# Moving GpSimd's products of a decoder mixer to VectorE and ScalarE, and the transfers around its triangular solves to ScalarE's queue

## The chip, the cores and the metric

The kernel runs on one core of one Trainium2 chip. Its time is the device time of one launch, in microseconds (us). The engines are named as in the profile: PE is TensorE (matmuls; PEld are its weight loads), DVE is VectorE, ACT is ScalarE, POOL is GpSimd and SP is SyncE, which issues DMA transfers.

## The reference

Two layers (`DEPTH`), 256 tokens, width 1024, f32. Each layer adds four sub-layers to x, each between an RMSNorm before and one after:

```python
x += 0.5 * post(SwiGLU_1(pre(x)))
x += post(W_out[ sum_i sigmoid(gate_i(h)) * U_i(branch_i(h)) ]),  h = pre(x)
#      branch A: latent attention with rotary keys (MLA), causal
#      branch B: gated linear attention (GLA), causal
#      branch C: RWKV-7 time mixing (a delta-rule state), causal
x += post(CrossAttn(pre(x), rmsnorm(mem)))
x += 0.5 * post(SwiGLU_2(pre(x)))
```

The change lies in the second sub-layer, the mixer. Its RWKV branch steps a state per head over the tokens:

```python
sa = state @ kk_t
state = state * w_t - sa x (kk_t * a_t) + v_t x k_t      # x: outer product
y_t = state @ r_t
```

Its GLA branch needs, for all j <= i, the product of q_i, k_j and a decay exp(b_i - b_j), with b a running sum of log gates.

## The kernel before, in words

All 256 tokens stay on the core as two halves of 128 (t = 0 and 1). Matmuls with weights are split in three: each weight block (tile `raw`, by DMA from SP's queue, three buffers) is cut on ACT into a high part (`whi`, a cast) and on DVE into the rest (`wlo`, a subtraction), eight tiles of each; every block then takes part in matmuls high x high, high x low and low x high. Intermediates lie in one big tile cut into buffers (`heap`; `heapr` for split activations; `small` for per-token numbers). PSUM has eight banks: `b_g` and `b_s` for projections and transposes, `b_ya` and `b_yb` for the branches.

Everything is recorded first: every operation becomes an entry of `Program.ops`, and so all compute instructions have the line of `issue` in the profile (L384). `Program.order` then plans: `cost` gives each operation a duration, `forward` simulates the five engines and takes at each one the ready operation of best rank, `backward` makes new ranks from the result, and the best plan of several rounds and passes is issued. The instruction order on every engine comes from these costs and rules, and the buffers in `heap` are laid by the planned times.

RWKV is done in chunks. `rwkv_keys` and `rwkv_products` form products of keys, decays and rates; `rwkv_front` forms, per half, the small matrices (matmuls of 64 contraction rows at two places of the array, `pe` = rows 0 to 63 or 64 to 127) and writes the triangular ones through DRAM (`sl`) into the layout of the solve (`XL`). `rwkv_solve` runs 31 steps on DVE, each a product (`tm`) and a subtraction (`xx`) over 248, 240, ..., 8 columns. The result goes out to DRAM in two layouts (`si`, `sx`) and back into `X1` and `XT`; `rwkv_back` multiplies it into the state. There are four solves: two halves in two layers.

GLA covers the causal triangle in seven levels of block size 64 down to 1 (`gla_attend`): two subtractions on DVE, an exponential on ACT, then the key product (128x256) and two query products into `zq` (64x256 each) on POOL, four matmuls, and an eviction by ACT or, for the four smaller and the last sizes, a predicated copy on DVE. RoPE (`rope`) takes four products and two sums per half. `branch` multiplies each branch's projection by its gate and adds it up (`mg`).

The FFN takes its outer factor 0.5 by a POOL operation on the gain `gb`; `meansq` computes 1/rms of a row.

Of the kernel before, what the change touches and what calls it, by code (L numbers as in the profile page):

```python
# [48 lines left out]
class Program:  # L49
# [139 lines left out]
    @staticmethod  # L189
    def columns(op):  # L190
# [10 lines left out]
    def order(self):  # L201

        self.preds = self.graph()
        ops = self.ops
        n = len(ops)
        self.eng = [o[0].name for o in ops]
        self.costs = [self.cost(o) for o in ops]
        self.succ = [[] for _ in range(n)]
        for i, p in enumerate(self.preds):
            for j in p:  # L210
                self.succ[j].append(i)
        self.size = [o[2][0].nbytes() / self.DMA_RATE if o[0].name == "sync" else 0.0 for o in ops]
# [15 lines left out]
        for i, users in enumerate(self.users):  # L228
            t = self.at[i]
            for b in users:  # L230
                b.start, b.end = min(b.start, t[0]), max(b.end, t[1] + (4.0 if self.eng[i] == "sync" else 0.2))
        return order

    def lag(self, i, s):
        if self.eng[i] == "sync":
            return self.DMA_START + self.size[i] + self.DMA_END
        return self.LAT[self.eng[i]][self.eng[i] != self.eng[s]]
# [36 lines left out]
    def forward(self, rank):  # L274
# [13 lines left out]
        parts, size, place, shared = self.parts, (128, 128), None, False  # L288
        while len(order) < n:
# [23 lines left out]
            if e == "tensor":  # L313
# [9 lines left out]
                if parts[i][0] != size:  # L323
                    j = min((x for x in ready[e] if parts[x[1]][0] == size and x[0] < rank[i] + self.STAY), default=None)
# [7 lines left out]
            if e == "tensor":  # L332
                if parts[i][0] != size:
                    size, shared = parts[i][0], False
                    c += self.DRAIN
                elif size != (128, 128) and not shared and any(
                        a != b for a, b, s in zip(parts[i][1], place, size) if s < 128):
                    shared = True
                    c *= 0.5
                else:  # L340
                    shared = False
# [6 lines left out]
            if e == "tensor":  # L348
# [5 lines left out]
                c *= 1 if warm else 2  # L354
            at[i] = (t, t + c)
# [3 lines left out]
            if e == "sync":  # L359
                dma_free = max(dma_free, t + self.DMA_START) + self.size[i]  # L360
                end = dma_free + self.DMA_END
                done.append(end)
            for s in self.succ[i]:
                rt[s] = max(rt[s], end if e == "sync" else end + self.LAT[e][e != eng[s]])
# [81 lines left out]
class Trunk:  # L446
# [397 lines left out]
    def postnorm(self, y, gb, t):  # L844

        jk, yg, ss = self.h.alloc(D), self.h.alloc(D), self.sm.alloc(2)
        self.meansq(y, jk, ss)
# [13 lines left out]
    def ffn(self, l, i, st, post_g, nxt, after_first=None):  # L861
# [46 lines left out]
        for c in range(1, NCH):  # L908
# [17 lines left out]
        for t in range(2):  # L926
# [3 lines left out]
            self.postnorm(ys[t], gb, t)  # L930
# [71 lines left out]
    def rwkv_keys(self, l):  # L1002
# [34 lines left out]
        for hp in range(4):  # L1037
            self.tt(kmv[:, hp, :], kmv[:, hp, :], k0[:, hp, :], MULT, nc.gpsimd)
        h.free(self.k0)
        for hp in range(4):  # L1040
            self.tt(aa[:, hp, :], aa[:, hp, :], kv[:, hp, :], MULT, nc.gpsimd)

    def rwkv_products(self, l):
# [5 lines left out]
        for hp in range(4):  # L1049
            self.tt(rv[:, hp, :], self.rr.v(f, b=4)[:, hp, :], self.km.v(f, b=4)[:, hp, :], MULT, nc.gpsimd)  # L1050
# [33 lines left out]
    def rwkv_front(self, l, t):  # L1084
# [51 lines left out]
        for q in range(4):  # L1136
            nc.sync.dma_start(sl[q * 8:q * 8 + 8].rearrange("h i j -> i h j"),
                              ln[32 * q:32 * q + 32, :, (q % 2) * 32:(q % 2) * 32 + 32])
        XL, XX = h.alloc(1024), h.alloc(256)
        nc.sync.dma_start(XL.ap, sl.rearrange("b i j -> b (i j)").unsqueeze(1).to_broadcast([32, 4, 1024]))  # L1140
        nc.sync.dma_start(XX.ap, self.ix)
        rt.update(MM=MM, mmv=mmv, PA=PA, BA=BA, pa=pa, ba=ba, LN=LN, ln=ln, XL=XL, XX=XX)

    def rwkv_solve(self, l, t):
# [15 lines left out]
        nc.sync.dma_start(si, XX.ap)  # L1160
        X1 = rt["X1"] = h.alloc(256)
        for q in (0, 2):
            nc.sync.dma_start(X1[32 * q:32 * q + 32, :].rearrange("p (b c) -> p b c", c=8),
                              si.rearrange("(q b) (i c) -> q i b c", q=4, c=8)[q])
        nc.scalar.copy(TM.v("p (c i) -> p c i", c=8), XX.v("p (i c) -> p c i", c=8))
        nc.sync.dma_start(sx, TM.ap)
        xt = XT.v("p (h n) -> p h n", h=8)
        sxv = sx.rearrange("(q h x) (c i) -> q (x c) h i", q=4, h=8, c=8)
        for q in range(4):
            nc.sync.dma_start(xt[32 * q:32 * q + 32, :, 32 * q:32 * q + 32], sxv[q])  # L1170
# [78 lines left out]
    def rwkv_out(self, l, och, ocl):  # L1249
# [7 lines left out]
        for t in range(2):  # L1257
# [11 lines left out]
            self.tt(Y.ap, Y.ap, lw, MULT, nc.gpsimd)  # L1269
            self.tt(Y.ap, Y.ap, lb, ADD, nc.gpsimd)  # L1270
# [3 lines left out]
            self.tt(Y.ap, Y.ap, VN.ap, ADD, nc.gpsimd)  # L1274
# [15 lines left out]
    def rope(self, dst, x1, x2, t, n, eng):  # L1290
# [50 lines left out]
    def mla_up(self, l):  # L1341
# [6 lines left out]
        for t in range(2):  # L1348
# [113 lines left out]
    def gla_attend(self, l, obh, obl):  # L1462
# [48 lines left out]
        for i, L in enumerate((64, 32, 16, 8, 4, 2, 1)):  # L1511
# [9 lines left out]
            self.tt(tv[:, :, 0, :], tv[:, :, 0, :], kv[:, :, 0, :], MULT, nc.gpsimd)  # L1521
            upat = "p (u b x n) -> p u b x n"
            tq, qq = (b.v(upat, u=4, x=2, n=L)[:, :, :, 1, :] for b in (T, QG))
            by_head(Z, lambda pe, z: self.tt(z.rearrange("p u (b n) -> p u b n", n=L), tq[pe], qq[pe], MULT, nc.gpsimd))
# [8 lines left out]
            else:  # L1533
# [19 lines left out]
        for t in range(2):  # L1553
# [13 lines left out]
            self.tt(ov, ov, self.p_gn.unsqueeze(1).to_broadcast([128, 4, 128]), MULT, nc.gpsimd)  # L1567
            self.tt(O.ap, O.ap, gg[t].ap, MULT, nc.gpsimd)
# [14 lines left out]
    def mixer(self, l, st, post_g, nxt):  # L1583
# [258 lines left out]
```

## Time and profile before

| | |
|---|---|
| time, three runs | 1681.28, 1686.76, 1687.56 us (median 1686.76) |
| the profiled execution | 1683.41 us, its span 1681.7 us |
| mean granted TensorE clock | 0.983 |
| busy: PE, DVE, ACT, POOL | 1602.7, 1105.1, 964.1, 268.4 us |
| instructions on POOL | 383 |
| transfers | 274.91 MB, mean 163 GB/s |

A row of a group of instructions names line, engine, operation, output and inputs, shape and count, then the busy time and the mean duration of one in ns, then the idle time of the engine before them and what ended it. A row of waits names who waited for whom, with total us, times and longest. A row of the timeline begins with start and duration in us; the idle time before it stands at its end. A row of a stretch gives the stretch, its length and each engine's busy time with the number of instructions. SPq is SP's queue.

### The profile page before, as it was taken

To read this page: it belongs to the slowest core of one execution; us is meant where nothing else is said; L and a number is where in the kernel's file an instruction comes from. 1 tells how busy PE (TensorE), PEld (TensorE's weight loads), DVE (VectorE), ACT (ScalarE), POOL (GpSimd) and SP (SyncE) were. 2 spreads that over 40 slices of the span, in tenths; PEclk is the share of its full clock that TensorE was granted. 3 is DMA by queue.
4 is the path that set the end of the run, shared out by engine and by line. 5 is a ranking of instruction groups with operands and counts; after the bars stand their busy time and mean duration, and the time that the engine had idled before them with its cause. 6 is when DMAs were issued, how large, how long until landed. Compare 5 with 4: busy or idle time off the path is not lost. (4 is left out here: it accounts for less than half of the span.)

```text
span 1681.7 us, 23946 instructions
## 1 busy us (share of the span) xinstructions
PE 1602.7 (95%) x8623; PEld 1337.0 (80%) x8623; DVE 1105.1 (66%) x1954; ACT 964.1 (57%) x1887; POOL 268.4 (16%) x383
## 2 busy tenths in 40 slices
PE   7999999998899999999999999999978999999998
PEld 5788798776677987888878887887766789878886
DVE  5555656958876667555675557676786776575555
ACT  5455675866445556555555556867854455564544
POOL 7000113105331101000010002310163320010000
PEclk9999999999999999999999999999988999999999
DMA  8655542522555635656555554443225555455652
GB/s 253 207 190 186 171 155 88 169 73 103 170 192 180 206 128 163 202 173 214 174 180 199 193 182 146 131 143 115 91 83 173 175 188 165 149 169 182 199 177 100
DMA packets 206091, 274.91 MB, mean 163 GB/s; under 512 B 28148, under 2 KB 157650, under 8 KB 205972
## 3 DMA queue, kind: packets, MB, share of 16 engines
q1 hardware_dynamic: 205972, 273.39, 50.0%
q8 instruction: 67, 1.10, 0.3%
q14 instruction: 52, 0.43, 0.1%
HBM read 270.60 MB, written 2.75 MB: 163 GB/s over the span
## 5 line engine op out<-in xcount | busy, mean ns | idle before, releaser
L384 DVE TENSOR_TENSOR wlo<-raw,whi 128x512 fp32r<-128x512 f32 (+1 forms) x964 | 673.5, 714 | 401.1 <-ACT whi L384 389.7
L384 ACT CAST whi<-raw 128x512 fp32r<-128x512 f32 (+1 forms) x964 | 582.4, 619 | 484.7 <-PE b_g L384 256.8
L384 PE MATMUL b_g<-whi,heapr 128*128 128x512 f32 (+2 forms) x1904 | 656.3, 405 | 15.8 <-DVE heap L384 5.5
L384 PEld LDWEIGHTS b_g<-whi,heapr 128*128 128x128 f32 x1904 | 357.4, 191 | 97.6 <-DVE heapr L384 7.3
L384 PE MATMUL b_g<-wlo,heapr 128*128 128x512 f32 (+2 forms) x952 | 369.3, 403 | 0.5 <-DVE wlo L384 0.4
L384 PEld LDWEIGHTS b_g<-wlo,heapr 128*128 128x128 f32 x952 | 181.5, 191 | 36.6 <-DVE wlo L384 2.3
L384 PE MATMUL b_g<-heapr,whi 128*128 128x256 f32 x1104 | 201.6, 290 | 2.8 <-DVE heap L384 2.8
L384 POOL TENSOR_SCALAR small<-small 128x1 f32<-128x1 f32 (+2 forms) x52 | 30.3, 583 | 987.4 <-ACT heap L384 962.7
L384 PE MATMUL b_ya<-whi,heapr 128*128 128x512 f32 x480 | 178.0, 394 | 0.2 <-ACT heapr L384 0.2
L384 PE MATMUL b_yb<-whi,heapr 128*128 128x512 f32 x480 | 174.6, 392 | 0.0
L384 PE MATMUL b_s<-whi,heapr 128*128 128x512 f32 x448 | 174.5, 399 | 0.0
L384 PEld LDWEIGHTS b_g<-heapr,whi 128*128 128x128 f32 x1104 | 166.2, 193 | 6.5 <-DVE heap L384 4.0
L384 POOL TENSOR_TENSOR heap<-heap 128x256 f32<-128x256 f32 (+2 forms) x85 | 101.8, 1208 | 207.7 <-DVE heap L384 105.5
L384 PE MATMUL b_g<-heapr,wlo 128*128 128x256 f32 x552 | 134.9, 290 | 0.0
L384 DVE TENSOR_TENSOR heap<-heap 128x512 f32<-128x512 f32 (+31 forms) x296 | 116.6, 406 | 15.8 <-PE b_yb L384 8.8
L384 PEld LDWEIGHTS b_yb<-whi,heapr 128*128 128x128 f32 x480 | 89.8, 188 | 18.9 <-DVE heapr L384 0.2
L384 PEld LDWEIGHTS b_ya<-whi,heapr 128*128 128x128 f32 x480 | 89.3, 188 | 19.2 <-ACT heapr L384 0.4
L384 PE MATMUL b_s<-ident,heap 128*128 128x128 f32 (+2 forms) x449 | 92.7, 275 | 10.1 <-DVE heap L384 8.4
L384 ACT CAST heapr<-b_s 128x256 fp32r<-128x256 f32 (+2 forms) x148 | 65.5, 444 | 58.2 <-PE b_s L384 50.8
L384 PEld LDWEIGHTS b_s<-whi,heapr 128*128 128x128 f32 x448 | 83.6, 188 | 18.4 <-DVE heap L384 0.6
L384 PEld LDWEIGHTS b_g<-heapr,wlo 128*128 128x128 f32 x552 | 96.2, 193 | 1.7 <-issue 1.0
L384 DVE TENSOR_TENSOR heapr<-b_s,heapr 128x256 fp32r<-128x256 f32 (+2 forms) x148 | 75.3, 509 | 33.6 <-ACT heapr L384 33.1
(163 smaller groups left out, 1692.3 us busy)
## 6 DMA issues: line engine op xcount, KB each, us to landing
raw<-in_w_ffn_in_dram SPq DMA_DIRECT2D x172, 512.0 KB, 4.9
raw<-in_w_in_dram SPq DMA_DIRECT2D x50, 1024.0 KB, 5.0
raw<-in_w_ffn_out_dram SPq DMA_DIRECT2D x44, 1024.0 KB, 6.9
raw<-in_mem_wkv_dram SPq DMA_DIRECT2D x16, 1024.0 KB, 6.0
raw<-in_w_branch_dram SPq DMA_DIRECT2D x12, 1024.0 KB, 5.3
raw<-in_w_out_dram SPq DMA_DIRECT2D x8, 1024.0 KB, 5.0
raw<-in_mem_wq_dram SPq DMA_DIRECT2D x8, 1024.0 KB, 4.8
raw<-in_mem_wo_dram SPq DMA_DIRECT2D x8, 1024.0 KB
```

The lines of the kernel that those rows point to most:

```text
L384: getattr(eng.real, method)(*a, **k)
```

## The change

Five things are edited.

1. The POOL products of the mixer (keys, RWKV products and output, RoPE, GLA levels and output, the sums of branches) become DVE operations; the copies of the identity into `MM` become one ACT copy for each solve.
2. The transfers of `sl`, `XL`, `XX`, `si`, `X1`, `sx` and `XT` are issued by ACT: 14 for each solve.
3. The factor 0.5 of the FFN leaves the POOL operation on `gb`; `postnorm` hands `over` = 2 to `meansq`, where it enters two constants.
4. The planner learns the new issuer (a transfer costs ACT 0.3), a port that DVE and POOL share (`shared`, `held`), and prices a small matmul at half wherever its place differs from that of the one before it; it takes such a one first.
5. Nothing else: the per-token reciprocal roots (`small`) and the zero fills stay on POOL.

```diff
+        if method == "dma_start":
+            return 0.3
...
+    def shared(op):
+        eng, method, a, k = op
+        if eng.name not in ("vector", "gpsimd") or method in ("memset", "iota"):
+            return False
+        out = k["out"] if "out" in k else a[0]
+        ins = [x for x in list(a) + list(k.values()) if isinstance(x, bass.AP) and x is not out and x.space != PSUM]
+        ins = [x for x in ins if int(np.prod(x.shape[1:])) > 1]
+        return len(ins) >= (2 if eng.name == "vector" else 1) or eng.name == "gpsimd"
...
+            if e == "gpsimd" and t < held["vector"]:
+                free[e] = held["vector"] + 0.03
+                continue
...
-                if parts[i][0] != size:
-                    j = min((x for x in ready[e] if parts[x[1]][0] == size and x[0] < rank[i] + self.STAY), default=None)
+                if parts[i][0] != size or size != (128, 128) and parts[i][1] == place:
+                    some = [x for x in ready[e] if parts[x[1]][0] == size and x[0] < rank[i] + self.STAY]
+                    j = min((x for x in some if parts[x[1]][1] != place), default=None)
+                    if not j and parts[i][0] != size:
+                        j = min(some, default=None)
...
-                elif size != (128, 128) and not shared and any(
-                        a != b for a, b, s in zip(parts[i][1], place, size) if s < 128):
-                    shared = True
+                elif place != parts[i][1]:
                     c *= 0.5
...
+            if e == "vector" and self.port[i]:
+                t = max(t, held["gpsimd"])
+            if e in held and self.port[i]:
+                held[e] = t + c
...
-    def meansq(self, halves, jk, ss):
+    def meansq(self, halves, jk, ss, over=1):
...
-            self.act(jk[:, hf * 512:hf * 512 + 512], halves[hf], AF.Square, scale=1.0 / 32, accum_out=ss[:, hf:hf + 1])
+            self.act(jk[:, hf * 512:hf * 512 + 512], halves[hf], AF.Square, scale=over / 32, accum_out=ss[:, hf:hf + 1])
...
-        g.tensor_scalar(ss[:, 0:1], ss[:, 0:1], ss[:, 1:2], EPS, ADD, ADD)
+        g.tensor_scalar(ss[:, 0:1], ss[:, 0:1], ss[:, 1:2], EPS * over * over, ADD, ADD)
...
-                self.nc.gpsimd.tensor_scalar(gb.ap, gb.ap, 0.5, 1.0, MULT, MULT)
...
-            self.tt(kmv[:, hp, :], kmv[:, hp, :], k0[:, hp, :], MULT, nc.gpsimd)
+            self.tt(kmv[:, hp, :], kmv[:, hp, :], k0[:, hp, :], MULT)
...
-        for u in range(0, 16, 4):
-            nc.gpsimd.tensor_copy(MM.v("p (u n) -> p u n", n=128)[0:64, u:u + 4, 0:64],
-                                  self.ident[0:64, 0:64].unsqueeze(1).to_broadcast([64, 4, 64]))
+        nc.scalar.copy(MM.v("p (u n) -> p u n", n=128)[0:64, :, 0:64], self.ident[0:64, 0:64].unsqueeze(1).to_broadcast([64, 16, 64]))
...
-        nc.sync.dma_start(XL.ap, sl.rearrange("b i j -> b (i j)").unsqueeze(1).to_broadcast([32, 4, 1024]))
-        nc.sync.dma_start(XX.ap, self.ix)
+        nc.scalar.dma_start(XL.ap, sl.rearrange("b i j -> b (i j)").unsqueeze(1).to_broadcast([32, 4, 1024]))
+        nc.scalar.dma_start(XX.ap, self.ix)
...
-        nc.sync.dma_start(si, XX.ap)
+        nc.scalar.dma_start(si, XX.ap)
...
-            self.tt(tv[:, :, 0, :], tv[:, :, 0, :], kv[:, :, 0, :], MULT, nc.gpsimd)
+            self.tt(tv[:, :, 0, :], tv[:, :, 0, :], kv[:, :, 0, :], MULT)
...
-            by_head(Z, lambda pe, z: self.tt(z.rearrange("p u (b n) -> p u b n", n=L), tq[pe], qq[pe], MULT, nc.gpsimd))
+            by_head(Z, lambda pe, z: self.tt(z.rearrange("p u (b n) -> p u b n", n=L), tq[pe], qq[pe], MULT))
...
-                        self.tt(mg[t][:, cc], mg[t][:, cc], gt[t][:, cc], ADD, nc.gpsimd)
+                        self.tt(mg[t][:, cc], mg[t][:, cc], gt[t][:, cc], ADD)
```

The same edit of one argument is made at the other products.

How the order changes is shown at three places; a row is one instruction or a run of equal ones, with its output, inputs and shape. First the GLA levels of layer 1. On POOL before, each level was a key product (for instance 128x8x32) and two query products into zq, one after the other:

```order
L384 TENSOR_TENSOR heap<-heap 128x4x64
L384 TENSOR_TENSOR zq_125<-heap 64x4x64 x2
L384 TENSOR_TENSOR heap<-heap 128x8x32
L384 TENSOR_TENSOR zq_126<-heap 64x4x64 x2
L384 TENSOR_TENSOR heap<-heap 128x16x16
L384 TENSOR_TENSOR zq_125<-heap 64x4x64 x2
```

Now they stand on DVE, between the steps of the second half's solve (128x184 to 128x160) and the subtractions of the next levels:

```order
L408 TENSOR_TENSOR heap<-heap 128x4x64
L408 TENSOR_TENSOR zq_125<-heap 64x4x64
L408 TENSOR_TENSOR heap<-heap 128x184
L408 TENSOR_TENSOR zq_125<-heap 64x4x64
L408 TENSOR_TENSOR heap<-heap 128x184
L408 TENSOR_TENSOR heap<-heap 128x16x16
L408 TENSOR_TENSOR heap<-heap 128x176
L408 TENSOR_TENSOR heap<-heap 128x8x32
L408 TENSOR_TENSOR heap<-heap 128x176
L408 TENSOR_TENSOR zq_126<-heap 64x4x64
```

One engine now holds the solve, the levels and the weight subtractions, which stood on two.

Second, the end of the last solve, layer 1. In SP's queue before, with weight loads (raw) ahead of and between the small transfers:

```order
L384 DMA raw_75<-in_w_in_dram 128x4x512
L384 DMA heap<-in_mem_norm_dram 128x1024
L384 DMA si_107<-heap 128x256
L384 DMA sx_106<-heap 128x256
L384 DMA raw_76<-in_w_in_dram 128x4x512
L384 DMA heap<-si_107 32x32x8
L384 DMA heap<-sx_106 32x8x32 x2
```

Now they stand in ACT's order, between its casts for the weights:

```order
L408 COPY heap<-heap 128x256
L408 DMA si_107<-heap 128x256
L408 DMA sx_106<-heap 128x256
L408 ACTIVATE heap<-b_g_64 128x512
L408 CAST whi_85<-raw_77 128x512
L408 DMA heap<-si_107 32x32x8
L408 DMA heap<-sx_106 32x8x32 x2
L408 DMA heap<-si_107 32x32x8
L408 DMA heap<-sx_106 32x8x32 x2
L408 CAST whi_78<-raw_75 128x512
```

The reads wait for the writes to land, and the casts behind them for the reads to be issued.

Third, PE in `rwkv_back` of layer 0, first half. The two banks b_ya_65 and b_ya_66 belong to the two places of the array. Before:

```order
L384 MATMUL b_ya_65<-heap 128x128 x4
L384 MATMUL b_ya_66<-heap 128x128 x4
L384 MATMUL b_g_64<-wlo_90,heapr 128x512
L384 MATMUL b_ya_65<-heap 128x128 x4
L384 MATMUL b_ya_66<-heap 128x128 x4
```

After:

```order
L408 MATMUL b_s_69<-ident,heap 128x128 x2
L408 MATMUL b_ya_65<-heap 128x128 x3
L408 MATMUL b_ya_66<-heap 128x128
L408 MATMUL b_ya_65<-heap 128x128
L408 MATMUL b_ya_66<-heap 128x128 x3
L408 MATMUL b_s_69<-ident,heap 128x128
L408 MATMUL b_g_63<-whi_80,heapr 128x512
L408 MATMUL b_ya_65<-heap 128x128 x2
L408 MATMUL b_ya_66<-heap 128x128
L408 MATMUL b_ya_65<-heap 128x128
```

Runs of four at one place have become shorter runs that change place more often.

More of the change, by code (lines that the diff above doesn't have):

```diff
@@ L189, in columns @@
     @staticmethod
+    def shared(op):
[6 more added lines that the diff above has]
+        return len(ins) >= (2 if eng.name == "vector" else 1) or eng.name == "gpsimd"
+    @staticmethod
     def columns(op):
@@ L211, in order @@
                 self.succ[j].append(i)
-        self.size = [o[2][0].nbytes() / self.DMA_RATE if o[0].name == "sync" else 0.0 for o in ops]
+        self.dma = [o[1] == "dma_start" for o in ops]
+        self.size = [o[2][0].nbytes() / self.DMA_RATE if d else 0.0 for o, d in zip(ops, self.dma)]
         self.cols = [self.columns(o) if o[0].name == "tensor" else 0.0 for o in ops]
         self.parts = [self.part(o) for o in ops]
+        self.port = [self.shared(o) for o in ops]
         rank, rest = [0.0] * n, 0.0
@@ L230, in order @@
             for b in users:
-                b.start, b.end = min(b.start, t[0]), max(b.end, t[1] + (4.0 if self.eng[i] == "sync" else 0.2))
+                b.start, b.end = min(b.start, t[0]), max(b.end, t[1] + (4.0 if self.dma[i] else 0.2))
         return order
     def lag(self, i, s):
-        if self.eng[i] == "sync":
+        if self.dma[i]:
             return self.DMA_START + self.size[i] + self.DMA_END
@@ L287, in forward @@
         at = [None] * n
-        parts, size, place, shared = self.parts, (128, 128), None, False
+        parts, size, place = self.parts, (128, 128), None
+        held = dict(vector=0.0, gpsimd=0.0)
         while len(order) < n:
@@ L333, in forward @@
                 if parts[i][0] != size:
-                    size, shared = parts[i][0], False
+                    size = parts[i][0]
                     c += self.DRAIN
-                elif size != (128, 128) and not shared and any(
-                        a != b for a, b, s in zip(parts[i][1], place, size) if s < 128):
-                    shared = True
+                elif place != parts[i][1]:
                     c *= 0.5
-                else:
-                    shared = False
                 place = parts[i][1]
@@ L362, in forward @@
                 done.append(end)
+            elif self.dma[i]:
+                end = t + self.DMA_START + self.size[i] + self.DMA_END
             for s in self.succ[i]:
-                rt[s] = max(rt[s], end if e == "sync" else end + self.LAT[e][e != eng[s]])
+                rt[s] = max(rt[s], end if self.dma[i] else end + self.LAT[e][e != eng[s]])
                 left[s] -= 1
@@ L842, in prenorm, with postnorm @@
             self.sm.free(ss)
-    def postnorm(self, y, gb, t):
+    def postnorm(self, y, gb, t, over=1):
         jk, yg, ss = self.h.alloc(D), self.h.alloc(D), self.sm.alloc(2)
-        self.meansq(y, jk, ss)
+        self.meansq(y, jk, ss, over)
         for hf, c in enumerate(self.halves):
@@ L929, in ffn @@
                 mms(t, hf, NCH - 1, w10)
-            self.postnorm(ys[t], gb, t)
+            self.postnorm(ys[t], gb, t, 2)
             nxt(t)
@@ L1037, in rwkv_keys @@
         for hp in range(4):
-            self.tt(kmv[:, hp, :], kmv[:, hp, :], k0[:, hp, :], MULT, nc.gpsimd)
+            self.tt(kmv[:, hp, :], kmv[:, hp, :], k0[:, hp, :], MULT)
         h.free(self.k0)
         for hp in range(4):
-            self.tt(aa[:, hp, :], aa[:, hp, :], kv[:, hp, :], MULT, nc.gpsimd)
+            self.tt(aa[:, hp, :], aa[:, hp, :], kv[:, hp, :], MULT)
     def rwkv_products(self, l):
@@ L1049, in rwkv_products @@
         for hp in range(4):
-            self.tt(rv[:, hp, :], self.rr.v(f, b=4)[:, hp, :], self.km.v(f, b=4)[:, hp, :], MULT, nc.gpsimd)
+            self.tt(rv[:, hp, :], self.rr.v(f, b=4)[:, hp, :], self.km.v(f, b=4)[:, hp, :], MULT)
         self.bon = self.sm.alloc(16)
@@ L1159, in rwkv_solve @@
             self.tt(xx[:, j + 1:32, :], xx[:, j + 1:32, :], tm[:, 0:n, :], SUB, eng)
-        nc.sync.dma_start(si, XX.ap)
+        nc.scalar.dma_start(si, XX.ap)
         X1 = rt["X1"] = h.alloc(256)
         for q in (0, 2):
-            nc.sync.dma_start(X1[32 * q:32 * q + 32, :].rearrange("p (b c) -> p b c", c=8),
+            nc.scalar.dma_start(X1[32 * q:32 * q + 32, :].rearrange("p (b c) -> p b c", c=8),
                               si.rearrange("(q b) (i c) -> q i b c", q=4, c=8)[q])
         nc.scalar.copy(TM.v("p (c i) -> p c i", c=8), XX.v("p (i c) -> p c i", c=8))
-        nc.sync.dma_start(sx, TM.ap)
+        nc.scalar.dma_start(sx, TM.ap)
         xt = XT.v("p (h n) -> p h n", h=8)
@@ L1169, in rwkv_solve @@
         for q in range(4):
-            nc.sync.dma_start(xt[32 * q:32 * q + 32, :, 32 * q:32 * q + 32], sxv[q])
+            nc.scalar.dma_start(xt[32 * q:32 * q + 32, :, 32 * q:32 * q + 32], sxv[q])
         h.free(XL, XX, TM)
@@ L1268, in rwkv_out @@
             self.tt(y, y, s.ap.unsqueeze(2).to_broadcast([128, 8, 64]), MULT)
-            self.tt(Y.ap, Y.ap, lw, MULT, nc.gpsimd)
-            self.tt(Y.ap, Y.ap, lb, ADD, nc.gpsimd)
+            self.tt(Y.ap, Y.ap, lw, MULT)
+            self.tt(Y.ap, Y.ap, lb, ADD)
             bo = self.bon[:, t * 8:t * 8 + 8]
@@ L1273, in rwkv_out @@
             self.tt(vn, vn, bo.unsqueeze(2).to_broadcast([128, 8, 64]), MULT)
-            self.tt(Y.ap, Y.ap, VN.ap, ADD, nc.gpsimd)
+            self.tt(Y.ap, Y.ap, VN.ap, ADD)
             ps = self.bank("ya")
@@ L1287, in rwkv_out, with rope @@
         sm.free(self.bon)
-    def rope(self, dst, x1, x2, t, n, eng):
+    def rope(self, dst, x1, x2, t, n):
         h = self.h
@@ L1296, in rope @@
         for j, (a, b) in enumerate(((x1, c), (x2, s), (x1, s), (x2, c))):
-            self.tt(tv[:, j], a, b, MULT, eng)
-        self.tt(dst[:, :, 0:16], tv[:, 0], tv[:, 1], SUB, eng)
-        self.tt(dst[:, :, 16:32], tv[:, 2], tv[:, 3], ADD, eng)
+            self.tt(tv[:, j], a, b, MULT)
+        self.tt(dst[:, :, 0:16], tv[:, 0], tv[:, 1], SUB)
+        self.tt(dst[:, :, 16:32], tv[:, 2], tv[:, 3], ADD)
         h.free(T)
@@ L1355, in mla_up @@
             q = qn[t].v(q3, h=8)
-            self.rope(q[:, :, 64:96], q[:, :, 64:80], q[:, :, 80:96], t, 8, nc.gpsimd)
+            self.rope(q[:, :, 64:96], q[:, :, 64:80], q[:, :, 80:96], t, 8)
         wk = self.wload([(0, self.kview(self.w["mla_w_ukv"][l]))], True)[0]
@@ L1361, in mla_up @@
             cr = c0[t].ap
-            self.rope(kr.ap.unsqueeze(1), cr[:, 384:400].unsqueeze(1), cr[:, 400:416].unsqueeze(1), t, 1, nc.gpsimd)
+            self.rope(kr.ap.unsqueeze(1), cr[:, 384:400].unsqueeze(1), cr[:, 400:416].unsqueeze(1), t, 1)
             self.tr(pr[:, t * 128:t * 128 + 128], kr.ap)
@@ L1542, in gla_attend @@
         self.act(T.ap, T.ap, AF.Exp)
-        self.tt(t2[:, :, 0:128], t2[:, :, 0:128], kg[:, :, 0:128], MULT, nc.gpsimd)
+        self.tt(t2[:, :, 0:128], t2[:, :, 0:128], kg[:, :, 0:128], MULT)
         by_head(Z, lambda pe, z: self.tt(z.rearrange("p (h x) n -> p h x n", h=2),
                                          t2[pe, :, 128:256].rearrange("p h (x n) -> p h x n", x=2),
-                                         qg[pe, :, 128:256].rearrange("p h (x n) -> p h x n", x=2), MULT, nc.gpsimd))
+                                         qg[pe, :, 128:256].rearrange("p h (x n) -> p h x n", x=2), MULT))
         ps = self.bank("yb", (2, 256))
@@ L1566, in gla_attend @@
             self.tt(ov, ps, ss.ap.unsqueeze(2).to_broadcast([128, 4, 128]), MULT)
-            self.tt(ov, ov, self.p_gn.unsqueeze(1).to_broadcast([128, 4, 128]), MULT, nc.gpsimd)
-            self.tt(O.ap, O.ap, gg[t].ap, MULT, nc.gpsimd)
+            self.tt(ov, ov, self.p_gn.unsqueeze(1).to_broadcast([128, 4, 128]), MULT)
+            self.tt(O.ap, O.ap, gg[t].ap, MULT)
             pt = self.bank("yb", (4, 128))
```

2 lines of the change are left out of this document (1 added, 1 removed).

## The prediction

> **What bounds the kernel now.** I read the page's first two sections, then busy times by stage, then the waits of TensorE, then single stretches.
>
> ```profile
> span 1681.7 us, 23946 instructions
> PE 1602.7 (95%) x8623; PEld 1337.0 (80%) x8623; DVE 1105.1 (66%) x1954; ACT 964.1 (57%) x1887; POOL 268.4 (16%) x383
> ...
> 160.00:200.00 40.00, 40.00 (x183) 32.67 (x183) 22.23 (x38) 20.08 (x40) 0.00 (x0) 1.00 0.59 189
> ...
> 200.00:520.00 320.00, 292.79 (x1817) 244.36 (x1816) 238.29 (x455) 202.66 (x406) 97.56 (x115) 0.97 0.43 137
> 520.00:1000.00 480.00, 478.57 (x2384) 400.20 (x2384) 297.15 (x489) 262.81 (x509) 22.95 (x28) 1.00 0.55 182
> 1000.00:1340.00 340.00, 308.76 (x1866) 258.93 (x1866) 242.67 (x462) 212.29 (x421) 93.62 (x113) 0.95 0.42 133
> ```
>
> The rows below the page's two lines give, after a stretch and its length, the busy time of PE, PEld, DVE, ACT and POOL, the granted clock, the DMA share and GB/s. TensorE is the bound: in an FFN stretch it runs 183 matmuls in 40.00 us, 0.22 us each, and in the FFN and cross-attention stage (520 to 1000) it stands still for 1.4 us of 480. In the two mixers (200 to 520, 1000 to 1340) it stands still for 27.2 + 31.2 = 58.4 us, at a clock of 0.97 and 0.95. POOL works almost only there. So only the mixers have something to give. Within them DVE is full while the triangular solves run:
>
> ```profile
> 297.50:333.80 36.30, 33.74 (x205) 27.73 (x204) 34.86 (x95) 30.86 (x72) 7.36 (x13) 1.00 0.50 166
> 381.90:451.50 69.60, 54.59 (x267) 44.37 (x266) 62.76 (x125) 37.54 (x62) 39.80 (x37) 0.90 0.35 117
> 1118.90:1155.40 36.50, 33.79 (x195) 29.61 (x194) 34.75 (x92) 28.64 (x60) 7.29 (x12) 1.00 0.49 165
> 1209.80:1279.90 70.10, 57.02 (x279) 47.22 (x278) 62.39 (x124) 39.43 (x64) 40.67 (x37) 0.93 0.32 103
> ```
>
> These are the four solves, first to last step. In the solve of the second token half (69.60 and 70.10 us, beside the GLA levels) DVE is busy 90% and 89%, TensorE loses 15.0 and 13.1 us. TensorE's own waits:
>
> ```profile
> PE b_yb L384 <- DVE heap L384: 13.4, 5, 6.0
> PE b_yb L384 <- POOL zq L384: 10.0, 6, 4.5
> PE b_ya L384 <- DMA heap<-sx: 5.8, 3, 4.1
> PE b_yb L384 <- POOL heap L384: 4.9, 4, 1.6
> ```
>
> POOL is named for 14.9 us, the reads that follow the solve for 5.8.
>
> **The moved products.** POOL's prices, one stall, and DVE's prices:
>
> ```profile
> L384 POOL TENSOR_TENSOR heap<-heap 128x512 f32<-128x512 f32 x32 | 50.0, 1567 | 104.8 <-DVE heap L384 100.7 <-DMA heap<-in_rwkv_ln_b_dram 3.4
> L384 POOL TENSOR_TENSOR heap<-heap 128x256 f32<-128x256 f32 x40 | 43.3, 1100 | 102.9 <-ACT heap L384 91.2 <-DVE heap L384 4.8 <-issue 4.8
> L384 POOL TENSOR_TENSOR zq<-heap 64x256 f32<-64x256 f32 x32 | 27.2, 849 | 1.2
> 1218.04 4.23 POOL L384 TENSOR_TENSOR heap<-heap 128x256 f32<-128x256 f32 x1 [17.63 <-ACT heap L384]
> 1223.80 2.08 PE L384 MATMUL b_yb<-zq,heap 128*128 128x128 f32 x8 [3.86 <-POOL zq L384]
> L384 DVE TENSOR_TENSOR heap<-heap,small 128x512 f32<-128x512 f32 x32 | 22.0, 688 | 3.0 <-POOL small L384 1.8 <-ACT heap L384 0.5
> L384 DVE TENSOR_TENSOR heapr<-b_s,heapr 128x256 fp32r<-128x256 f32 x96 | 40.3, 420 | 14.2 <-ACT heapr L384 13.7
> L384 DVE TENSOR_TENSOR heap<-b_ya,mask 64x256 f32<-64x256 f32 x32 | 13.4, 419 | 0.4
> L384 DVE TENSOR_TENSOR heap<-heap 128x184 f32<-128x184 f32 x8 | 4.8, 598 | 0.2
> L384 DVE TENSOR_TENSOR heap<-heap 128x232 f32<-128x232 f32 x8 | 3.2, 395 | 0.1
> L384 DVE TENSOR_TENSOR heap<-heap 128x136 f32<-128x136 f32 x8 | 2.4, 294 | 0.1
> L384 DVE TENSOR_TENSOR heap<-heap 128x64 f32<-128x64 f32 x8 | 1.8, 220 | 0.1
> 381.90:451.50 69.60, 21.06 (x50) 10.26 (x51) 22.32 (x26) 0.90 0.35 117
> ```
>
> The two engines hold each other up. A 128x256 product of 1.10 us took 4.23 us on POOL while DVE ran a row of products, and TensorE stood 3.86 us behind it. DVE's step on 184 columns (598 ns) is dearer than that on 232 (395 ns), because it ran beside POOL. The last row is of the wlo subtractions alone in one solve stretch: 26 took 22.32 us, 858 ns each, where a clean 128x512 takes 688.
>
> DVE gets 36 products of 512 columns (four of them by the norm gain in pb), 40 of 256, 32 of 64x256 into zq, and 48 small ones of RoPE: 24 of 128 columns, at most the 0.294 of 136, and 24 of 16, at most the 0.22 of 64: 36 x 0.688 + 40 x 0.42 + 32 x 0.42 + 24 x 0.294 + 24 x 0.22 = 67.4 us. Pricing DVE's present instructions at clean rows like these, I estimate 45 to 55 us of lock time that it loses today and gets back. Its total hardly moves; what matters is where.
>
> Solve stretch of the second half: added are 8 products of 256, 16 into zq and 3 of 512 = 8 x 0.42 + 16 x 0.42 + 3 x 0.69 = 12.1 us; returned is an estimated 9 us, half of it wlo's (26 x 0.17 = 4.4). From the order of the two programs, 28 and 33 wlo tiles are made within it where 25 stood: 3 and 8 more. DVE's work becomes 62.8 - 9 + 12.1 + 2.1 = 68.0 and 62.4 - 9 + 12.1 + 5.5 = 71.0 us. Today DVE idles 7 us there; with 4 to 5 us of idling left the stretches last 72.5 and 75.5 us, 2.9 and 5.4 longer. But each more weight tile feeds six matmuls of 0.22 us, 1.3 us: 3.9 and 10.5 us more TensorE work in them. Net -1.0 and -5.1, **-6.1**; between +3 (DVE idles as long as now) and -13 (it never idles).
>
> Solve stretch of the first half: DVE is at 96% and 95% and takes 12 RoPE products, 3.5 us, longer each; but RoPE's POOL chain held TensorE up (most of the 4.9). **+1**, between -3 and +6.
>
> Hidden work: the identity copies (16 on POOL become 4 on ACT), since their buffer is read only after the solve; without that cover, four copies of about 1.0 us. The halved FFN gain, four POOL operations that waited for a DMA; its factor moves into two constants. Here nothing is late.
>
> **TensorE's order.** The planner now alternates small matmuls between halves of the array.
>
> ```profile
> 273.19 1.71 PE L384 MATMUL b_ya<-heap 64*128 64x128 f32 x16
> ```
>
> Eight matmuls in two passes each, four at one place and then four at the other: 1.71 us, 16 passes nearly one after the other. There are 16 such groups, with one change of place each. In the new order I count 72 changes where 112 would alternate throughout; (72-16)/(112-16) = 0.58. If alternation halves a group (no row shows one; the ends are no gain and 0.86 us), 0.58 x 16 x 0.86 = 8.0; I take **-6**, as the single change in each group visibly overlaps; between 0 and -8.
>
> **The small transfers.**
>
> ```profile
> 1194.83 1.79 SPq L384 DMA_DIRECT2D sl<-heap  x4
> 1203.29 0.40 SPq L384 DMA_DIRECT2D raw<-in_w_branch_dram  x1
> 1203.92 0.53 SPq L384 DMA_DIRECT2D heap<-sl  x1
> ...
> 333.99 0.34 SPq L384 DMA_DIRECT2D si<-heap  x1
> ...
> 335.77 0.93 SPq L384 DMA_DIRECT2D heap<-si  x2
> 336.88 2.04 SPq L384 DMA_DIRECT2D heap<-sx  x4
> ...
> 1278.30 0.37 SPq L384 DMA_DIRECT2D raw<-in_w_in_dram  x1
> 1280.08 0.42 SPq L384 DMA_DIRECT2D si<-heap  x1
> 1286.09 0.32 SPq L384 DMA_DIRECT2D heap<-si  x1
> sl<-heap SPq DMA_DIRECT2D x16, 32.0 KB, 3.3
> 1209.79 0.87 DVE L384 TENSOR_TENSOR heap<-heap 128x248 f32<-128x248 f32 x2 [1.65 <-DMA heap<-sl]
> ```
>
> The read of sl stood in SP's queue behind a weight load that waited for a free buffer: 7.3 us after the last write (1196.6), of which 3.3 are landing, so 4.0 lost per layer. After the solve si took 6.0 us to land right behind a 1024 KB load, 1.8 where none was near. PE's 5.8 us for sx are mostly this; of them I take 5, and half of the 2 x 4.0, as DVE waited only 1.65 us of it: **-9**, between 0 and -14.
>
> By the Trainium skill, "DMA: Bandwidth & Descriptors", section "Issuing engines are not separate DMA queues", transfers from different engines end on the same 16 DMA engines and interleave, and a second issuer saves only issue time. No run here shows it yet, since all transfers are SP's; by it the landing part stays, and the gain would be 5 us smaller.
>
> What is late next: ACT. It issues 14 transfers per solve, 56 in all; four cost SP 2.04 us, 0.5 each, so 28 us more on ACT, and each dependent read also holds the casts behind it until its write lands.
>
> ```profile
> L384 ACT CAST whi<-raw 128x512 fp32r<-128x512 f32 x940 | 570.0, 621 | 472.2 <-PE b_g L384 245.0 <-PE b_yb L384 98.2 <-PE b_s L384 42.6
> ```
>
> Mostly ACT's casts wait for TensorE to free a tile, so ACT runs ahead by up to eight tiles: **+3**, between 0 and +25. TensorE's clock: with shorter waits some of its half-speed spells go, **-3**, between 0 and -6.
>
> Sum: -6.1 + 1 - 6 - 9 + 3 - 3 = -20.1. The profiled execution took 1683.4 us, so 1663.3, say 1663. The three runs shown have a median of 1686.8, 3.4 above it; 0.5% (8.4 us) is about what a measurement of this kernel can tell from no change.
>
> **Rivals.** (a) DVE takes POOL's place as the bound: both solve stretches go to their bad ends, +3 and +6 in place of -6.1 and +1. For it: 89 to 96% busy. Against: the lock time it gets back. Sum -6 + 9 - 9 + 3 - 3 = -6: 1677, no change.
> (b) Slower, by ACT's queue: in each solve the sl read waits about 2.7 us behind one cast (3.3 less 0.6), the si and sx reads 3 to 4 us, and 14 issues take 7: 13 us, 52 for four solves. If TensorE runs dry for all of it the sum is -23.1 + 52 = +28.9, 1712; it decides from 23 of the 52 on, and at 36 gives 1696. For it: ACT also evacuates PSUM and makes GLA's exponentials there. Against: the row above. The same page ("Anatomy of one DMA") says that a wait for a semaphore is made on the issuing sequencer before dispatch; that is how SP behaved at 1286.09.
> (c) In another queue the transfers land no sooner, and only the place behind the blocked weight load is gained: the DMA term is -4 and the time 1668, still faster. For it: si took its 6.0 us while 1024 KB of weights were under way, and those stay under way. Against: 1.8 beside 6.0 us within one queue says that order in the queue matters. The Trainium skill's page named above gives this.
>
> **Chances.** The forecast 0.54, (a) 0.18, (b) 0.12, (c) 0.16. Faster by over 0.5%: 0.54 + 0.16 and the better part of (a), 0.05, make 0.75; same 0.13, the rest of (a); slower 0.12, (b). The range reaches down by the good ends of the second solve, transfers and clock (-6.9, -5, -3) and RoPE's -4 and alternation's -2 to 1642, rounded to 1640, and up past (a) into the mild half of (b), 1685.
>
> **What the profile after would show.** TensorE's waits: no line with POOL zq or heap. POOL's 268 less 120 for the three groups above and the smaller ones, about 110; DVE near 1115, its wlo near 0.69 us. Stretches of the second solve 70 to 76 us with more matmuls. Groups of eight near 1.2 us. si landing in 2 to 4 us; PE's wait for sx below 2. ACT's casts waiting on transfers would show (b). Wrong it would be above all if TensorE's waits for POOL come back as waits for DVE of the same length.

## The result, and the profile after

The changed kernel takes **1658.2 us** (median of 4 runs, 1655.9 to 1660.0) against 1685.8 before (4 runs, 1681.3 to 1687.6): a ratio of 0.984, interval 0.982 to 0.986, or 27.6 us less. The forecast was 1663. The total came out near it, but two of its terms were far off in opposite directions, as the experiments show.

First the page's two lines of the profiled execution after, then busy times by stretch (stretch and length, then PE, PEld, DVE, ACT and POOL with their counts, clock, DMA share, GB/s). The stretches are the two mixers and the four solves, first to last step; the last two rows are of the `wlo` subtractions alone.

```profile
span 1654.2 us, 23796 instructions
PE 1592.2 (96%) x8623; PEld 1327.5 (80%) x8623; DVE 1102.5 (67%) x2110; ACT 969.3 (59%) x1891; POOL 111.7 (7%) x207
...
200.00:507.00 307.00, 287.69 (x1821) 240.10 (x1819) 238.73 (x531) 207.95 (x410) 20.64 (x29) 0.98 0.45 143
987.00:1312.00 325.00, 302.58 (x1854) 252.45 (x1854) 239.96 (x535) 210.04 (x419) 24.36 (x31) 0.96 0.43 136
293.50:329.70 36.20, 34.60 (x218) 28.95 (x217) 34.85 (x109) 31.81 (x72) 0.52 (x1) 1.00 0.48 157
375.70:438.40 62.70, 58.40 (x302) 47.04 (x302) 60.87 (x156) 44.11 (x71) 5.00 (x6) 1.00 0.40 132
1103.50:1139.60 36.10, 34.32 (x215) 28.93 (x215) 34.93 (x108) 31.02 (x71) 0.52 (x1) 1.00 0.41 135
1189.70:1257.60 67.90, 63.16 (x330) 50.15 (x329) 64.58 (x163) 50.99 (x85) 6.92 (x4) 1.00 0.41 131
...
375.70:438.40 62.70, 24.63 (x62) 11.68 (x62) 19.12 (x29) 1.00 0.40 132
1189.70:1257.60 67.90, 25.61 (x66) 12.24 (x65) 22.52 (x34) 1.00 0.41 131
```

TensorE's idle time in the mixers fell from 58.4 us to 19.3 + 22.4 = 41.7. DVE does 156 more instructions in less busy time than before (1102.5 against 1105.1 us). In the second-half solves it is now busy 97% and 95%, more than before, and still the stretches are shorter (62.7 and 67.9 us) with 35 and 51 more matmuls in them; their granted clock is 1.00, where it was 0.90 and 0.93. The cause stands in the groups of instructions (the first row is of before):

```profile
L384 DVE TENSOR_TENSOR wlo<-raw,whi 128x512 fp32r<-128x512 f32 x940 | 659.5, 717 | 390.5 <-ACT whi L384 379.1 <-PE b_ya L384 3.1 <-PE b_s L384 0.6
...
L408 DVE TENSOR_TENSOR wlo<-raw,whi 128x512 fp32r<-128x512 f32 x940 | 634.5, 690 | 379.7 <-ACT whi L408 371.5 <-issue 0.6 <-PE b_g L408 0.2
L408 DVE TENSOR_TENSOR heap<-heap 128x256 f32<-128x256 f32 x70 | 27.8, 421 | 5.5 <-ACT heap L408 4.9
L408 DVE TENSOR_TENSOR zq<-heap 64x256 f32<-64x256 f32 x32 | 13.3, 417 | 0.3
L408 DVE TENSOR_TENSOR heap<-heap 128x184 f32<-128x184 f32 x8 | 2.8, 344 | 0.1
```

The moved products cost 421 and 417 ns each, as estimated; the 184-column step fell from 598 to 344 ns, below that on 232 columns (396), where it belongs; `wlo` fell from 717 to its clean 690. TensorE's waits show the other side:

```profile
PE b_s L408 <- DVE heap L408: 10.5, 3, 5.7
PE b_ya L408 <- DMA heap<-sx: 9.9, 2, 6.0
...
PE b_yb L408 <- DVE heap L408: 3.5, 8, 0.9
...
PE b_yb L408 <- DVE zq L408: 1.9, 4, 1.1
```

The lines with POOL (14.9 us) are gone and came back as 1.9 for DVE's `zq`; the wait for DVE's `heap` in `b_yb` fell from 13.4 to 3.5. The longest line, `b_s` for DVE's `heap` (8.4 before), lies at the start of the kernel and of the two mixers, not at the solves. But the wait for the transfer `sx`, which was to fall below 2 us, rose from 5.8 to 9.9. The timeline after the last solve, of ACT, its queue (ACTq) and PE:

```profile
1257.60 0.34 ACTq L408 DMA_DIRECT2D si<-heap  x1
1258.33 0.34 ACTq L408 DMA_DIRECT2D sx<-heap  x1
1259.21 0.61 ACT L408 CAST whi<-raw 128x512 fp32r<-128x512 f32 x1
1263.41 0.33 ACTq L408 DMA_DIRECT2D heap<-si  x1
...
1265.72 3.49 ACTq L408 DMA_DIRECT2D heap<-sx  x2
1269.26 1.66 ACT L408 CAST whi<-raw 128x512 fp32r<-128x512 f32 x3 [9.43 <-DMA heap<-si]
...
1262.72 0.62 PE L408 MATMUL b_g<-whi,heapr 128*128 128x512 f32 x2
1269.32 1.15 PE L408 MATMUL b_ya<-heap 32*32 32x32 f32 x32 [5.98 <-DMA heap<-sx]
```

`si` is issued at 1257.60; ACT makes one more cast, which ends at 1259.8, and stands before the dependent read until `si` has landed, 5.8 us after its issue. That is 3.6 us of standing; issuing the six reads then takes another 5.8, until 1269.2, and the next cast comes 9.43 us after the last. TensorE had weight matmuls until 1263.3; the next in its order need `sx`, and it stood 5.98 us.

### The profile page after: what moved, and what is told of

It reads as the page before. It is cut to its first block, busy times and chain, and to the rows that moved or that the text cites. A ratio compares the mean times of both kernels' runs of the same rounds, so it can differ in the third digit from the quotient of the medians.

```text
span 1654.2 us, 23796 instructions
## 1 busy us (share of the span) xinstructions
PE 1592.2 (96%) x8623; PEld 1327.5 (80%) x8623; DVE 1102.5 (67%) x2110; ACT 969.3 (59%) x1891; POOL 111.7 (7%) x207
## 4 chain that ended last, share of the span: by engine, by line
PE 75%; DVE 12%; ACT 5%; DMA 4%; issue 2%; POOL 0%; SPq 0%; ACTq 0%; DVEq 0%; POOLq 0%
PE b_g L408 40%; PE b_ya L408 14%; PE b_s L408 11%; PE b_yb L408 10%; DVE heap L408 5%; DVE wlo L408 4%; ACT heap L408 3%; DMA raw<-in_w_ffn_in_dram 1%; ACT whi L408 1%; ACT L408 1%; DMA raw<-in_w_ffn_out_dram 1%; DVE small L408 1%; DVE heapr L408 1%; DMA heap<-sx 1%; DMA si<-heap 1%
## 5 line engine op out<-in xcount | busy, mean ns | idle before, releaser
L408 DVE TENSOR_TENSOR wlo<-raw,whi 128x512 fp32r<-128x512 f32 (+1 forms) x964 | 648.4, 688 | 389.2 <-ACT whi L408 381.1
L408 DVE TENSOR_TENSOR heap<-heap 128x256 f32<-128x256 f32 (+29 forms) x376 | 129.0, 364 | 15.2 <-DMA heap<-in_rwkv_ln_w_dram 5.2
L408 PE MATMUL b_ya<-heap 64*128 64x128 f32 (+5 forms) x776 | 82.3, 278 | 12.3 <-DMA heap<-sx 9.9
```

The costliest lines, as they stand in the source:

```text
L408: getattr(eng.real, method)(*a, **k)
```

## The experiments

All were timed in five rounds against the kernel before on the same chip, and the ratios are to it. That kernel took 1682.2 to 1685.3 us beside them, so times of different rows compare to within about 3 us.

| edit | us | ratio, interval |
|---|---|---|
| before + products on DVE | 1653.2 | 0.981, 0.979 to 0.983 |
| before + transfers in ACT's queue | 1693.9 | 1.006, 1.004 to 1.009 |
| after, products on POOL again | 1672.6 | 0.993, 0.991 to 0.995 |
| after, old pairing | 1658.0 | 0.984, 0.982 to 0.986 |
| after, planned landing + 3 us | 1665.3 | 0.990, 0.988 to 0.991 |
| after, only the reads in SP's queue | 1641.0 | 0.975, 0.974 to 0.977 |
| **after, all transfers in SP's queue (S)** | **1640.0** | 0.974, 0.972 to 0.976 |
| S + old pairing | 1640.9 | 0.974, 0.973 to 0.976 |
| S + idle copies of products on POOL | 1663.1 | 0.989, 0.987 to 0.990 |
| S without the port rule | 1646.3 | 0.978, 0.976 to 0.980 |
| S + gain and identity copies on POOL | 1645.0 | 0.977, 0.975 to 0.980 |
| S, one planner number moved (control) | 1638.9 | 0.973, 0.971 to 0.975 |

**The products alone.** All `nc.gpsimd` arguments of the mixer are dropped in the kernel before.

```diff
-            self.tt(tv[:, :, 0, :], tv[:, :, 0, :], kv[:, :, 0, :], MULT, nc.gpsimd)
+            self.tt(tv[:, :, 0, :], tv[:, :, 0, :], kv[:, :, 0, :], MULT)
```

> The kernel before with the products and RoPE on VectorE and nothing else. If the products carry the gain: 1655 to 1662, wlo near 0.69 us. By the forecast's terms (8 us): about 1677. If VectorE becomes the bound (rival a): 1685 or slower, with TensorE waiting for VectorE as long as it waited for POOL.

31.0 us less than the 1684.2 of before: the products alone do more than the whole change. The page, DVE's group and one wait:

```profile
PE 1594.9 (97%) x8623; PEld 1328.7 (81%) x8623; DVE 1101.4 (67%) x2110; ACT 966.7 (59%) x1887; POOL 124.2 (8%) x227
...
L384 DVE TENSOR_TENSOR wlo<-raw,whi 128x512 fp32r<-128x512 f32 x940 | 634.8, 690 | 372.9 <-ACT whi L384 366.4
...
PE b_yb L384 <- DVE zq L384: 1.6, 4, 0.5
```

DVE takes 156 instructions more and is 3.7 us less busy. Rival (a), DVE as the new bound, is out. (The second-half solves last 76.1 and 77.6 us here, longer than before, with 39 `wlo` tiles made in each where 26 were: the length of a stretch alone says little.)

**The products undone in the changed kernel** (the same edit backwards).

> The changed kernel with the 172 products and RoPE back on POOL; the transfers, the pairing and the missing gain operation stay. If nearly all of the gain came from the products (POOL's waits and the lock on DVE): 1683 or more, wlo near 0.72 us again, TensorE waiting for POOL 10 to 15 us. By the forecast's terms (solve stretches and clock, 8 us): about 1666.

(156 products went back, RoPE's 48 among them; the 172 of the expectation is a miscount.) Between the two: 14.4 us slower. POOL's groups, DVE's and TensorE's waits:

```profile
L408 POOL TENSOR_TENSOR zq<-heap 64x256 f32<-64x256 f32 x32 | 36.9, 1153 | 27.8 <-PE b_yb L408 26.6
...
L408 DVE TENSOR_TENSOR wlo<-raw,whi 128x512 fp32r<-128x512 f32 x940 | 647.9, 705 | 394.3 <-ACT whi L408 387.1 <-PE b_g L408 0.2
...
PE b_yb L408 <- POOL zq L408: 9.0, 4, 3.6
PE b_yb L408 <- DVE heap L408: 7.2, 1, 7.2
```

The waits for POOL return, but `wlo` only rises to 705 ns, where before had 717, while POOL's `zq` products are now 1153 ns against 849. That fits the planner's new rule, which makes POOL give way to DVE; no run tests it. The products' worth thus depends on the rest: 31 us under the old rule and in SP's queue, 14 under the new one and in ACT's.

**POOL work that nobody waits for.** S, in which POOL repeats the key and query products of the seven levels into a buffer that nobody reads (`S` in the code, not the kernel S); TensorE and DVE never wait for its values.

```diff
+            self.tt(S.v(pat, x=2, n=L)[:, :, 0, :], tv[:, :, 0, :], kv[:, :, 0, :], MULT, nc.gpsimd)
+            by_head(S.ap, lambda pe, z: self.tt(z.rearrange("p u (b n) -> p u b n", n=L), tq[pe], qq[pe], MULT, nc.gpsimd))
```

> The changed kernel with the small transfers in SP's queue (1640 us), in which POOL also repeats 42 GLA products of the seven levels into a buffer that nobody reads; TensorE never waits for POOL's result. If POOL's products cost by holding VectorE up: wlo in the second solves back at 0.78 us or more, 1648 to 1655. If they cost only as slow links of the chain that TensorE waited for: within 3 us of 1640.

23.1 us slower than S. POOL's two groups, two of DVE's, and TensorE's wait; then the same two DVE groups and the wait in S:

```profile
L408 POOL TENSOR_TENSOR heap<-heap 64x256 f32<-64x256 f32 x28 | 26.1, 932 | 1.9
L408 POOL TENSOR_TENSOR heap<-heap 128x256 f32<-128x256 f32 x14 | 12.9, 919 | 96.7 <-DVE heap L408 96.2
L408 DVE TENSOR_TENSOR zq<-heap 64x256 f32<-64x256 f32 x32 | 18.9, 592 | 0.4
L408 DVE TENSOR_TENSOR heap<-heap 128x104 f32<-128x104 f32 x8 | 3.0, 376 | 0.0
PE b_yb L408 <- DVE zq L408: 13.5, 8, 4.1
```

```profile
L408 DVE TENSOR_TENSOR zq<-heap 64x256 f32<-64x256 f32 x32 | 13.3, 416 | 0.3
L408 DVE TENSOR_TENSOR heap<-heap 128x104 f32<-128x104 f32 x8 | 2.1, 258 | 0.0
PE b_yb L408 <- DVE zq L408: 1.0, 4, 0.3
```

42 POOL operations, 39.0 us of them, make DVE 13.9 us busier (1116.6 against 1102.7) and TensorE's wait for `zq` 12.5 us longer. The expectation missed in two points: the time lies beyond its 1655, and `wlo` stayed at 691 ns; the load fell on other operations of DVE. The run also does not price the port alone. The copies keep each level's buffer in use for longer, and the planner, which knows the port, made another order: the second-half solves last 50.5 and 57.2 us here, 76.3 and 71.8 in S. What part of the 23 us is the port is open. The Trainium skill ("SBUF — State Buffer", "SBUF: two separate sides") says that DVE, where it has two inputs in SBUF, and a GpSimd operation that reads SBUF exclude each other: whichever starts first holds the shared ports for its whole instruction. 416 against 592 ns for the same product agrees.

**The transfers.** S is the changed kernel with one word changed seven times in `rwkv_front` and `rwkv_solve`:

```diff
-        nc.scalar.dma_start(si, XX.ap)
+        nc.sync.dma_start(si, XX.ap)
```

> The changed kernel with all 14 small transfers per solve back in SP's queue, nothing else. Forecast's step (the move gains 9 us): about 1667 and TensorE's wait for sx back near 5.8 us or more. Rival 1 (only the place behind the blocked weight load counted, gain 4): about 1662. Rival 2, from the trace after, where TensorE's waits for sx grew from 5.8 to 9.9 us and ACT's casts stood 9.4 us behind si and 6.6 behind sx: the move cost some 4 to 8 us, and this kernel is faster, 1650 to 1654.

18.2 us **faster** than the changed kernel, more than rival 2 of this expectation said. SP's queue, ACT and TensorE's wait in S:

```profile
330.61 0.34 SPq L408 DMA_DIRECT2D si<-heap  x1
332.39 0.92 SPq L408 DMA_DIRECT2D heap<-si  x2
...
452.20 0.46 SPq L408 DMA_DIRECT2D si<-heap  x1
459.98 0.32 SPq L408 DMA_DIRECT2D heap<-si  x1
...
458.55 0.62 ACT L408 CAST whi<-raw 128x512 fp32r<-128x512 f32 x1
459.51 0.63 ACT L408 CAST whi<-raw 128x512 fp32r<-128x512 f32 x1 [0.34 <-PE b_g L408]
...
PE b_ya L408 <- DMA heap<-sx: 3.7, 2, 2.2
```

By the issue of the first read, `si` lands in 1.8 us once and in 7.8 another time: SP's queue is no surety for a short landing (from ACT's queue the writes of the four solves took up to 3.2, 4.0, 4.0 and 5.8). But in those 7.8 us ACT goes on casting, and TensorE has work until 460.3. Between the two profiled executions lie 14.6 us; TensorE's wait for `sx` makes 6.2 of them (9.9 against 3.7), and the rest is spread over its other waits, such as that of `b_g` for ACT's `heap` (6.4 against 2.9).

The transfers alone, in the kernel before, with the planner's lines for them:

> The kernel before with the 56 small transfers in ACT's queue (and the planner's lines that allow it), nothing else. Forecast's steps (-9 for the transfers, +3 for ACT's issues): 6 us faster, 1678. If the move costs what the run with the transfers back in SP's queue showed on the changed kernel (18 us): 1702. If the slower solves of this kernel hide part of that: 1685 to 1695.

11.6 us slower, as in the expectation's last case: the move loses there too, in the direction of rival (b).

Reads and writes apart: `XL`, `XX`, `X1` and `XT` in SP's queue, `sl`, `si` and `sx` written from ACT's.

> The changed kernel with the writes of sl, si and sx in ACT's queue and the reads (XL, XX, X1, XT) in SP's. If the cost is ACT standing at the reads: 1640 to 1645, like the kernel with all of them in SP's queue. If it is the issue time on ACT (24 of 56 issues stay there): about 1650. If it is the landing of transfers among the weight loads: 1640 to 1643 as well, with TensorE's wait for sx near 4 us.

1641.0, the same as S, with TensorE waiting 5.4 us for `sx`, more than in S. So the whole cost comes with the reads in ACT's queue, none with the 24 writes, and TensorE's own wait for the data is not its measure. All reads but that of `XX` wait for a transfer to land. Whether ACT's standing until then costs the time, or the issuing of the reads itself, no run separates; some issues are long. The reads of `sx` in the changed kernel and in S (shortest, median and longest issue in ns), and TensorE's wait in this run:

```profile
L408 ACTq DMA_DIRECT2D heap<-sx x16: 325/564/3306, 333.1 to 1268.7; - x16
...
L408 SPq DMA_DIRECT2D heap<-sx x16: 319/452/1899, 333.4 to 1268.9; - x16
...
PE b_ya L408 <- DMA heap<-sx: 5.4, 3, 3.4
```

The planner told that those transfers land later:

```diff
+                end = t + self.DMA_START + self.size[i] + self.DMA_END + 3.0
```

> The changed kernel, transfers in ACT's queue, but the planner counts 3 us more for the landing of those transfers (4 to 6 us, as measured, in place of its 2 to 3), so that it sets casts ahead of the reads. If the cost of the ACT queue is ACT standing at a read that has not landed: 1641 to 1648, ACT's casts no longer waiting for si or sx (9.4 and 6.6 us before). If it is the 56 issues themselves (about 28 us of ACT): no change, 1658. If it is that the transfers land late for TensorE whatever stands ahead: about 1655, waits for sx near 10 us.

7 us slower than the changed kernel, against all three cases of the expectation. ACT and PE in the last solve:

```profile
1278.36 0.60 ACT L408 ACTIVATE heap<-b_g 128x512 f32<-128x512 f32 x1 [6.90 <-DVE heap L408]
1279.01 0.80 PE L408 MATMUL b_g<-whi,heapr 128*128 128x512 f32 x1 [5.24 <-ACT heap L408]
PE b_g L408 <- ACT heap L408: 14.2, 8, 6.2
```

The waits for `sx` are gone, but in the new order ACT stands 6.90 us before an activation that DVE releases, with the casts behind it, and TensorE again stands. Why the order came out so is open; the run does not tell what a landing planned right would be worth.

**TensorE's pairing.** The old choice and price in the changed kernel and in S:

```diff
-                if parts[i][0] != size or size != (128, 128) and parts[i][1] == place:
+                if parts[i][0] != size:
```

> The changed kernel with the old choice among small matmuls (it no longer prefers the other half of the array). Forecast's step: 6 us slower, 1664. By the trace after, where the 64-row group's busy time fell from 29.9 to 26.5 us: 3 us slower, 1661. If alternation is worth nothing: 1658.

> The changed kernel with the small transfers in SP's queue (1640 us) and the old choice among small matmuls. Forecast's step (alternation is worth 6 us): 1646. By the run of the old choice on the changed kernel itself, where nothing changed: 1640. Since the planner sets the whole order anew, a spread of some 3 us is no answer either way.

1658.0 against 1658.2, and 1640.9 against 1640.0: worth nothing that shows. Two groups of eight in the changed kernel, and the whole kind in it and with the old choice:

```profile
458.80 1.16 PE L408 MATMUL b_ya<-heap 64*128 64x128 f32 x16
342.40 1.76 PE L408 MATMUL b_ya<-heap 64*128 64x128 f32 x16
L408 PE MATMUL b_ya<-heap 64*128 64x128 f32 x256 | 26.5, 285 | 0.0
```

```profile
L409 PE MATMUL b_ya<-heap 64*128 64x128 f32 x256 | 31.0, 285 | 1.0 <-ACT heap L409 0.5 <-DVE heap L409 0.4
```

Five groups of eight now take 1.16 us, where 1.71 was usual before; others take up to 2.3. That the fast ones are those whose places alternate throughout is likely but not shown, since the trace does not name the places. The 4.5 us of busy time saved against the old choice do not reach the end.

**What else is in it.** The kernel with only the products (1653.2) is 13.2 us above S. Besides the pairing, three edits lie between: the port rule (here every operation's `port` is set to False), and the gain and identity copies (here back on POOL).

> The changed kernel with the small transfers in SP's queue (1640 us), whose planner knows nothing of VectorE and POOL holding each other up. It ran 13 us less than the kernel with only the products moved, and this is one of four differences between the two. If the planner's rule makes the 13 us: 1650 or more. If, with POOL's products gone, the rule has little left to order: within 3 us of 1640.

> The changed kernel with the small transfers in SP's queue (1640 us), with the halving of the FFN gain and the identity copies back on POOL: the other two of the four differences to the kernel with only the products moved. Forecast's step (both hidden): 1640. If they make the 13 us, by holding VectorE up beside the solves: 1650 or more.

6.3 and 5.0 us slower than S. Since every edit sets the order anew, a control:

> A control: the changed kernel with the small transfers in SP's queue (1640 us) and one number of the planner, which no other text speaks of, moved by 2% (KEEP from 4500 to 4600), so that the whole order is set anew as much as by the edits of the other runs. If the 5 and 6 us of the two runs before are more than chance among orders: within 2 us of 1640. If orders scatter by that much: anywhere between 1634 and 1650, and those two terms stay open.

1.1 us from S. Four orders of nearly the same program lie between 1638.9 and 1641.0, so 5 and 6 us look like more than the chance of an order; but each median is known to some 3.5 us either way, and both terms are at the edge of what these rounds tell. By which waits they act was not followed up.

## Why the prediction was right, and where it was not

- **Solve stretches of the second half, -6.1: right in mechanism, far too small.** They run 6.9 and 2.2 us shorter. Of the 35 and 51 more matmuls in them, 34 and 25 are weight matmuls of 0.22 us, 7.5 and 5.5 us more work; the others are small and not counted here. That makes -14.4 and -7.7, together -22.1, and TensorE's idle time in them fell from 15.0 + 13.1 to 4.3 + 4.7 us, by 19.1. Both lie beyond the bound of -13. (The two bounds do not follow from the prediction's own numbers: its 68.0 and 71.0 us of work make about -15 where DVE never idles and -1 where it idles 7 us.) The mis-sized step is the returned time: 62.76 + 12.1 + 3 x 0.69 = 76.9 us of work became 60.87, and 62.39 + 12.1 + 8 x 0.69 = 80.0 became 64.58: 16.1 and 15.4 us returned, where 9 each was estimated. Over the kernel 1105.1 + 67.4 - 1102.5 = 70.0 us came back by the prediction's price of the moved products (whose terms sum to 67.3), against 45 to 55. DVE also idles only 1.8 and 3.3 us, not 4 to 5. The 3 and 8 more `wlo` tiles were right (26 and 26 became 29 and 34).
- **Solve stretches of the first half, +1: wrong sign, and small.** They last 36.2 and 36.1 us, 0.1 and 0.4 less, and TensorE's idle time in them fell from 2.6 + 2.7 to 1.6 + 1.8 us. The kinds of matmuls in them changed too, so the term is not known more closely.
- **Alternation, -6: nothing.** The fastest groups gained 0.55 us, not the 0.86 estimated; many gained nothing; and undoing it changed neither kernel's time.
- **Small transfers, -9, and ACT's issues, +3: wrong in sign, +18.2 in place of -6.** The step that failed is that 5 of PE's 5.8 us for `sx` would go: in the last solve `si` landed in 5.8 us from ACT's queue and in 6.0 from SP's before, as rival (c) said. The bound of +25 held, but the cover named for it did not: ACT was thought up to eight tiles ahead, and after its last cast TensorE had weight matmuls for 3.5 us (1259.8 to 1263.3), under three tiles at 1.3 us, of a hold of 9.4 us. Rival (b) had the mechanism, standing and issuing together; its priced 52 us were about three times too many. The Trainium skill ("DMA: Bandwidth & Descriptors", "Issuing engines are not separate DMA queues") says that transfers of all issuing engines run on the same 16 DMA engines, and that a second issuer saves only issue time. The landings agree; a saving of issue time does not show here.
- **Gain and identity copies, 0: roughly -5.0 by the last experiments.** The planner's port rule, which had no term, roughly -6.3.
- **Clock, -3:** the mean went from 0.983 to 0.987, and to 0.990 in S; in the second-half solves it went from 0.90 and 0.93 to 1.00. Its worth is not separable from the shorter waits.

By the runs: products -31.0, port rule -6.3, copies -5.0, pairing 0, transfers +18.2, together -24.1 where -27.6 was measured (interval of the ratio: -31 to -23). The parts do not simply add up: undone in the changed kernel, the products are worth 14.4, not 31.0. Against their terms the products were 25.9 us better (-31.0 for -6.1 + 1), the transfers 24.2 worse and the pairing 6 worse, and 11.3 came from edits that had been put at nothing: the total was right by luck, by errors that cancelled.

## What to carry to other kernels

When two engines hold each other up, price a move by the engine that stays: its own instructions get cheaper, and a full engine may take work and finish sooner. Do not put a transfer that waits for another transfer into the queue of an engine that feeds TensorE; the write may go there, the dependent read belongs to a queue where nothing useful stands behind it. A total that comes true proves no term: undoing each part alone showed that the best kernel here (1640 us, 2.6% below before) is the change without its move of the transfers.

## What the runs showed of the hardware

- 39.0 us of POOL products that nobody reads made DVE 13.9 us busier; the kernel, in another order, was 23.1 us slower.
- A 128 KB write of `si` landed in 1.7 to 7.8 us in SP's queue within one execution, beside weight loads; from ACT's queue it took up to 5.8.
- Issuing one 32 KB read of `sx` took 0.33 to 3.31 us in ACT's queue (median 0.56) and 0.32 to 1.90 in SP's (median 0.45).
- 16 passes of 64 contraction rows usually took 1.71 us where four matmuls at one place followed four at the other; in the new order five such groups took 1.16.
